# Layer 0's last stage: p is loaded, turned and split within the down-projection's last steps, and gates are closed one block product into the next group

## The chip, the core and the metric

The kernel runs on one core of one Trainium2 chip. The metric is the device time of one execution in microseconds. A second figure, the span, is the time from the first to the last instruction that the profile of one execution shows; a little time lies around it.

## What is computed

Two layers of a decoder trunk, for 512 tokens of 1024 features, all in float32. Each layer mixes tokens, then applies a gated MLP with a short convolution, and ends with an embedding that is added for each layer. The change lies at the seam of the last two parts of layer 0:

```python
def _conv_ffn(h, w_up, conv_w, conv_b, w_down):
    u = _causal_depthwise_conv(h @ w_up, conv_w) + conv_b
    gate, up = jnp.split(u, 2, axis=-1)
    return (jax.nn.gelu(gate, approximate=False) * up) @ w_down

def _per_layer_embedding(x, p_i, norm, w_gate, w_proj):
    gate = jax.nn.sigmoid(_rms_norm(x, norm) @ w_gate)
    return gate * (p_i @ w_proj)

# in the loop over the layers i
    x = x + _conv_ffn(_rms_norm(x, ffn_norm[i]), ffn_w_up[i], ffn_conv_w[i], ffn_conv_b[i], ffn_w_down[i])
    x = x + _per_layer_embedding(x, p[i], ple_norm[i], ple_w_gate[i], ple_w_proj[i])
```

Here `w_down` is 2816 x 1024, `w_gate` 1024 x 1024, `w_proj` 256 x 1024, and `p[i]` 512 x 256.

## The kernel before, in words

**Layout.** The residual x lies transposed in SBUF, as eight blocks `xT[m]` of 128 features by 512 tokens. Every product is made of float32 numbers cut in two: a high part (ScalarE copies to the rounded type fp32r) and the rest (VectorE subtracts). A product then takes three matmuls, high by high, high by low and low by high (`mm3`, lines 165 to 171, or the inner `product` of `seven`, lines 884 to 886). The helpers of such cuts are `split` (lines 108 and 109, or 111 and 112 with a gain), `cut` (149 and 150) and `cut_blocks` (825 and 826).

**Order.** The kernel is written for a framework whose planner lays out each engine's queue. Under `manual_schedule(engines={ET.PE})` TensorE's queue keeps the written order. The queues of VectorE, ScalarE, GpSimd and SP are ordered by the planner, which gives the earlier written instruction the preference among those whose inputs and buffers it expects to be ready. `high_priority(offset=n)` moves a block of instructions n places forward in that preference. Each queue then runs strictly in its order. Buffers belong to tags with a fixed number of slots: `raw` (fresh weights, 2 slots), `wh` and `wl` (cut weights, 3 each), `R` (2), `four` (7), `rs` (4), and two sets of PSUM banks, `ps` and `pa`, of 4 each. A load into a slot waits until the last reader of the slot's old contents is through.

**Block products.** A 2 x 2 product of blocks is done with seven half-sized products instead of eight (`seven`, line 870). One call handles a pair of output blocks X and Y, each 128 features by 512 tokens, and is a generator: TensorE's program takes it up to a `yield` and may put other work there. In order: W (weights `plain`, operand `e1`), copied by ScalarE into the left halves of X and Y (lines 890, 891); V (`t13`, `s1`), copied out by line 897 when asked; `o1` into X's left half and `s2` (weights `t2`) into Y's left half; a copy to X's right half (line 900); `s3` into it; a copy to Y's right half (line 903); `s4` into Y and `o2` into X. Each of the seven has 12 matmuls of 128 x 256. The weights' forms are made by `seven_forms` in this order: `plain` is cut (line 843); two subtractions (849, 850); `t13` is cut; a subtraction (857); `t2` is cut at a preference 40 places forward, into the `sq` slots that the sums of squares use; a subtraction (860). The last form is cut in `seven` itself (line 901).

**The down-projection** (`down`, line 1116) runs a plan of 16 steps for layer 0. The last two (steps 14 and 15 of 0 to 15) are the products of output blocks 6 and 7 with three activation blocks each: 18 matmuls of 128 x 512 a step. Then line 1210 adds the banks to `xT[6]` and `xT[7]`, and `finish` calls `blocks` (line 293), which scales each block by the norm's gain (299), cuts it, forms the sums that `seven` needs (314 to 318), cuts those, and adds the block's squares to the norm's sum (290, 291).

**The embedding of layer 0** (`ple0`, line 1311) follows. p is loaded in two halves into `R` slots (`p_halves`, line 1289, issued on SP); one of these slots holds the low part of activation block 7 until step 13 of the down-projection has used it. Then come the load of gate group 0's weights (line 1323), its forms, the load of the projection's weights into a `raw` slot (line 1336) and their split in two column halves (line 1339). Under the manual order for TensorE stand `load_p` (eight transposes of p, line 1305, and two splits of the result, called pT), the products `proj(0)` and `proj(1)`, and the loop over four gate groups of two feature blocks each. Group g issues the load of group g + 1, runs the seven products, and puts between them: in group 0 `end_norm` (line 333: transposes of the squares, line 330, a sum, line 339, and a reciprocal root on GpSimd, line 179) and `spread` (line 343: four transposes, line 348, and a copy, line 350, which make R); in the others two `proj`. Then it closes the gates: three VectorE operations with R (lines 1385, 1387, 1388), and for each block a sigmoid (1391), a product with proj (1392), an addition to `xT` (1393) and the squares. In the last group `enter` cuts the finished blocks for layer 1's first product. Layer 1's mixer follows.

The short lines that a sentence can't carry, of the loop before the change:

```python
                next(steps)
                if g == 0:
                    R = self.spread()
                else:
                    pjs.append(proj(2 * g + 1))
                last = steps
                if not ends:
                    steps = prepare(raw)
                X, Y, more = next(last)
```

Of the kernel before, what the change touches and what calls it, by code (L numbers as in the profile page):

```python
# [14 lines left out]
AF = mybir.ActivationFunctionType  # L15
ALU = mybir.AluOpType
# [3 lines left out]
P = 128  # L20
# [43 lines left out]
class Kernel:  # L64
# [802 lines left out]
        left, right = HALVES  # L867
        return dict(e1=part(0, left), o1=part(1, left), o2=part(1, right), s1=s1, s2=s2, s3=s3, s4=s4)

    def seven(self, od, ws, x, keep=None):  # L870


        nc = self.nc
        H = S // 2
        mm = nc.tensor.matmul
        W, V = self.pa(), self.pa()[:, :H]
        X, Y = self.ps(), self.ps()
        plain, t13, t2 = ws

        def product(out, w, c, x, first=False):  # L880
            kw = dict(skip_group_check=True)
            for j in range(ND // 2):
                (wh, wl), (xh, xl) = w(j, c), x(j)
                mm(out, wh, xh, start=first and j == 0, stop=False, **kw)  # L884
                mm(out, wh, xl, start=False, stop=False, **kw)  # L885
                mm(out, wl, xh, start=False, stop=j == ND // 2 - 1, **kw)  # L886

        left, right = HALVES
        product(W[:, left], plain, 0, x["e1"], True)
        nc.scalar.copy(X[:, left], W[:, left])  # L890
        nc.scalar.copy(Y[:, left], W[:, left])
        yield
        product(V, t13, 0, x["s1"], True)
        more = V
        if keep is not None:
            more = keep()
            nc.scalar.copy(more, V)
        product(X[:, left], plain, 1, x["o1"])
        product(Y[:, left], t2, 0, x["s2"])
        yield nc.scalar.copy(X[:, right], Y[:, left])  # L900
        last = self.cut_blocks(od)
        product(X[:, right], t13, 1, x["s3"])
        yield nc.scalar.copy(Y[:, right], X[:, right])
        product(Y[:, left], last, 1, x["s4"])
        product(X[:, right], last, 0, x["o2"])
        yield X, Y, more

    def ffn(self, i, project, next_gain):


        nc, a, tc = self.nc, self.a, self.tc
# [5 lines left out]
        with tc.tile_pool(name=f"ffn{i}", bufs=1) as fp:  # L917
            self.mlp = fp
            kept, acts, fours = [None] * NF, [None] * NF, []
# [104 lines left out]
            down_forms = []  # L1024
# [23 lines left out]
            operands = self.tokens_and_forms(xg, self.forms)  # L1048
# [8 lines left out]
            with tc.manual_schedule(engines={ET.PE}):  # L1057
                late = begin(0, steps, w0c)
                close = lambda: None
                for d in range(groups):  # L1060
                    g, y = both(), both()
                    copied = next(steps)
# [6 lines left out]
                    copied = next(steps)  # L1069
# [37 lines left out]
            work = [lambda f=f: split_blocks(f) for f in (14, 16, 18, 20)]  # L1107
            for f in (8, 10, 12):
                split_pair(f)
            self.down(i, acts, down_forms, both, work, finish, copied)  # L1110
            if i == 0:
                self.ple0(fp, both, self.g_mix[1])
            else:
                self.ple1(fp)

    def down(self, i, acts, forms, both, work, finish, copied):


        nc, tc = self.nc, self.tc
        H = S // 2  # L1120
# [190 lines left out]
    def ple0(self, fp, both, next_gain):  # L1311


        nc, a, tc = self.nc, self.a, self.tc
        H = S // 2
        forms = self.forms
        wg = a["ple_w_gate"][0].rearrange("(k p) n -> p k n", p=P)
        operands = {q: (lambda j, q=q: forms[j][q]) for q in ("e1", "o1", "o2", "s1", "s2", "s3", "s4")}
        groups = ND // 2

        def load(g):
            raw = self.raw(ND, 2 * P)
            nc.sync.dma_start(raw, wg[:, :, 2 * P * g : 2 * P * (g + 1)])
# [12 lines left out]
        nc.sync.dma_start(wj_raw, a["ple_w_proj"][0].rearrange("(k p) n -> p k n", p=P))  # L1336
        wj = [self.four(fp).rearrange("p a b -> p (a b)").rearrange("p (k n) -> p k n", k=2) for _ in range(2)]
        for c in (slice(0, D // 2), slice(D // 2, D)):
            self.split([w[:, :, c] for w in wj], wj_raw[:, :, c])

        def proj(m):
            pj = self.pa()
            c = slice(m * P, (m + 1) * P)
            for k in range(2):
                self.mm3(pj, [w[:, k, c] for w in wj], pT[k], start=k == 0, stop=k == 1)
            return pj

        def enter(*ms):
            for m in ms:
                hl = self.pair(self.fp, "b0", "b1")  # L1350
                self.split(hl, self.xT[m], next_gain[:, m : m + 1])
                self.xg.append(hl)

        with tc.manual_schedule(engines={ET.PE}):
            pT = self.load_p(0, fp, pin)
            pjs = [proj(0), proj(1)]
            for g in range(groups):
                ends = g + 1 == groups
                if not ends:
                    raw = load(g + 1)  # L1360
                next(steps)
                if ends:
                    enter(0, 1)
                next(steps)
                if ends:
                    enter(2, 3)
                if g == 0:
                    self.end_norm()
                    self.begin_norm(None)
                else:  # L1370
                    pjs = [proj(2 * g)]
                next(steps)
                if g == 0:
                    R = self.spread()
                else:
# [8 lines left out]
                h2 = lambda x: x.rearrange("p (u t) -> p u t", u=2)  # L1384
                nc.vector.tensor_tensor(gates[:, 0], X, R, ALU.mult)
                s = gates[:, 1]
                nc.vector.tensor_tensor(h2(s), h2(Y), more.unsqueeze(1).to_broadcast([P, 2, H]), ALU.add)
                nc.vector.tensor_tensor(s, s, R, ALU.mult)
                for c in range(2):
                    m, s = 2 * g + c, gates[:, c]  # L1390
                    nc.scalar.activation(s, s, AF.Sigmoid)
                    nc.vector.tensor_tensor(s, s, pjs[c], ALU.mult)
                    nc.vector.tensor_tensor(self.xT[m], self.xT[m], s, ALU.add)
                    self.squares(m)
            enter(6, 7)
        self.end_norm()

# [650 lines left out]
```

## Time and profile before

| what | value |
|---|---|
| median of 3 runs | 1211.22 us (1210.53 to 1211.4) |
| the profiled execution's own time | 1211.32 us |
| its span | 1209.5 us, 20223 instructions |
| mean granted TensorE clock | 0.996 |
| TensorE (matmul) busy | 1192.0 us, 99% |
| VectorE busy | 993.3 us, 82% |
| ScalarE busy | 691.6 us, 57% |
| GpSimd busy | 45.3 us, 4% |
| DMA | 117.76 MB, mean 97 GB/s |

How to read it. The profile calls TensorE PE (and its weight loads PEld), VectorE DVE, ScalarE ACT, GpSimd POOL and SyncE SP. "L1305" is line 1305 of the kernel. "out<-in" names tiles by the program's names, so `ps` and `pa` are PSUM banks and `wh<-raw` is a cut of fresh weights. Times in the timeline count from the span's start. An entry such as "[3.95 <-ACT four L108]" says that the engine sat idle for 3.95 us before this instruction, and that what ended the wait was ScalarE's instruction of line 108 that writes a tile `four`. The granted clock is the share of TensorE's full clock that the chip allowed. Matmuls are pipelined, so the step from one start to the next is what a matmul costs, not its own length. The seam that the change touches lies at 500 to 600 us.

### The profile page before, as it was taken

How to read it: one execution, taken by the hardware profiler on the slowest of the kernel's cores; microseconds unless marked ns; L12 is line 12 of the kernel's file. 1: busy time of each engine (PE TensorE's matmuls, PEld its weight loads, DVE VectorE, ACT ScalarE, POOL GpSimd, SP SyncE). 2: the span in 40 equal slices, each digit the busy share in tenths (PEclk: the TensorE clock that was granted, in tenths of full speed). 3: DMA queues.
4: the chain of work that ended last, by engine and by line, in shares of the span. 5: the costliest groups of instructions: out<-in, count | busy, mean ns of one | idle time of the engine just before them, and what ended most of it. 6: DMA issues, size and time to landing. Idle time of an engine off the chain costs nothing.

```text
span 1209.5 us, 20223 instructions
## 1 busy us (share of the span) xinstructions
PE 1192.0 (99%) x8218; PEld 1081.0 (89%) x8218; DVE 993.3 (82%) x1593; ACT 691.6 (57%) x1135; POOL 45.3 (4%) x64
## 2 busy tenths in 40 slices
PE   9999999999999999979999999999999999999998
PEld 8887789999999889859978988889999999888887
DVE  6786687898999986868769876687989999988595
ACT  7466565655565644745673564555565656645374
POOL 2600000000000000000100000000000000000000
PEclk9999999999999999989999999999999999999999
DMA  7232222323232433231321322223333333422601
GB/s 221 76 101 70 73 88 70 120 91 119 92 110 83 148 122 96 67 108 61 114 93 47 93 71 70 87 70 105 106 105 105 103 107 97 139 88 96 209 1 70
DMA packets 112928, 117.76 MB, mean 97 GB/s; under 512 B 2840, under 2 KB 107858, under 8 KB 112836
## 3 DMA queue, kind: packets, MB, share of 16 engines
q1 hardware_dynamic: 112000, 115.88, 29.8%
q8 instruction: 64, 1.05, 0.4%
q0 software_dynamic: 560, 0.42, 0.3%
q14 instruction: 28, 0.23, 0.1%
q10 hardware_dynamic: 276, 0.18, 0.0%
HBM read 114.37 MB, written 2.10 MB: 96 GB/s over the span
## 4 chain that ended last, share of the span: by engine, by line
PE 60%; issue 29%; DVE 7%; ACT 2%; DMA 1%; POOL 0%; ACTq 0%; POOLq 0%; DVEq 0%
PE ps L169 10%; PE ps L171 10%; PE ps L170 10%; PE pa L170 4%; PE pa L171 4%; PE pa L169 4%; PE ps L884 3%; PE ps L886 3%; PE ps L885 3%; DVE wl L150 1%; PE ps L1446 1%; PE ps L1445 1%; PE ps L1444 1%; PE pa L886 1%; DVE wl L826 1%
## 5 line engine op out<-in xcount | busy, mean ns | idle before, releaser
L150 DVE TENSOR_TENSOR wl<-raw,wh 128x1024 fp32r<-128x1024 f32 (+4 forms) x142 | 163.0, 1149 | 41.6 <-ACT wh L149 41.1
L149 ACT ACTIVATE wh<-raw 128x1024 fp32r<-128x1024 f32 (+4 forms) x142 | 141.4, 998 | 87.1 <-PE ps L170 55.5
L825 ACT ACTIVATE wh<-raw 128x1024 fp32r<-128x1024 f32 x90 | 95.8, 1065 | 125.1 <-DVE raw L850 76.1
L826 DVE TENSOR_TENSOR wl<-raw,wh 128x1024 fp32r<-128x1024 f32 x90 | 110.2, 1224 | 28.9 <-ACT wh L825 28.8
L938 DVE SCALAR_TENSOR_TENSOR zt<-z,vfa,zt 128x510 f32<-128x510 f32 (+1 forms) x176 | 131.2, 746 | 0.3
L171 PE MATMUL pa<-b,wl 128*128 128x256 f32 x352 | 97.3, 276 | 0.1
L171 PE MATMUL pa<-a,wl 128*128 128x256 f32 x352 | 97.3, 276 | 0.0
L169 PE MATMUL pa<-a,wh 128*128 128x256 f32 x352 | 97.2, 276 | 0.0
L170 PE MATMUL pa<-b,wh 128*128 128x256 f32 x352 | 97.2, 276 | 0.0
L169 PE MATMUL pa<-b,wh 128*128 128x256 f32 x352 | 97.2, 276 | 0.0
L170 PE MATMUL pa<-a,wh 128*128 128x256 f32 x352 | 97.2, 276 | 0.0
L936 ACT ACTIVATE zt<-z,vfb 128x512 f32<-128x512 f32 x88 | 71.6, 813 | 18.6 <-DVE z L928 9.3
L169 PE MATMUL ps<-b,wh 128*128 128x512 f32 x192 | 76.6, 399 | 0.0
L170 PE MATMUL ps<-b,wh 128*128 128x512 f32 x192 | 75.1, 391 | 0.0
L171 PE MATMUL ps<-b,wl 128*128 128x512 f32 x192 | 75.0, 390 | 0.0
L171 PEld LDWEIGHTS pa<-b,wl 128*128 128x128 f32 x352 | 66.1, 188 | 0.2 <-DVE wl L150 0.2
L169 PEld LDWEIGHTS pa<-b,wh 128*128 128x128 f32 x352 | 66.1, 188 | 0.0
L170 PEld LDWEIGHTS pa<-a,wh 128*128 128x128 f32 x352 | 66.1, 188 | 0.0
L170 PEld LDWEIGHTS pa<-b,wh 128*128 128x128 f32 x352 | 66.1, 188 | 0.0
L169 PEld LDWEIGHTS pa<-a,wh 128*128 128x128 f32 x352 | 66.1, 188 | 0.0
L171 PEld LDWEIGHTS pa<-a,wl 128*128 128x128 f32 x352 | 66.1, 188 | 0.0
L884 PE MATMUL ps<-four,wh 128*128 128x256 f32 x232 | 64.7, 279 | 0.0
(470 smaller groups left out, 3769.2 us busy)
## 6 DMA issues: line engine op xcount, KB each, us to landing
raw<-in_ffn_w_up_dram SPq DMA_DIRECT2D x42, 1024.0 KB, 5.0
raw<-in_ffn_w_down_dram SPq DMA_DIRECT2D x13, 1024.0 KB, 5.4
raw<-in_hy_w_in_dram SPq DMA_DIRECT2D x8, 1024.0 KB, 5.2
raw<-in_gla_w_in_dram SPq DMA_DIRECT2D x8, 1024.0 KB, 5.2
raw<-in_ffn_w_down_dram SPq DMA_DIRECT2D x8, 768.0 KB, 4.9
raw<-in_ple_w_gate_dram SPq DMA_DIRECT2D x6, 1024.0 KB, 5.2
raw<-in_hy_w_out_dram SPq DMA_DIRECT2D x16, 256.0 KB, 4.2
raw<-in_gla_w_out_dram SPq DMA_DIRECT2D x4, 1024.0 KB, 5.0
```

The costliest lines, as they stand in the source:

```text
L149: nc.scalar.activation(hv, v, AF.Copy)
L150: self.rest_cut = nc.vector.tensor_tensor(lv, v, hv.bitcast(F32), ALU.subtract)
L169: mm(out, lh, rh, start=start, stop=False, **kw)
L170: mm(out, lh, rl, start=False, stop=False, **kw)
L171: mm(out, ll, rh, start=False, stop=stop, **kw)
L825: nc.scalar.activation(h, src, AF.Copy)
L826: nc.vector.tensor_tensor(l, src, h.bitcast(F32), ALU.subtract)
L884: mm(out, wh, xh, start=first and j == 0, stop=False, **kw)
L885: mm(out, wh, xl, start=False, stop=False, **kw)
L886: mm(out, wl, xh, start=False, stop=j == ND // 2 - 1, **kw)
L936: nc.scalar.activation(y, z, AF.Identity, scale=w2[:, f : f + 1], bias=bb[:, f : f + 1])
L938: nc.vector.scalar_tensor_tensor(out=y[:, tap:], in0=z[:, : S - tap], scalar=w[:, f : f + 1], in1=y[:, tap:], op0=ALU.mult, op1=ALU.add,)
```

## The change

Four things are done, all in layer 0.

- The load of p is called at the beginning of step 14 of the down-projection, and the transposes and splits of p, with them a Sigmoid of four columns into a spare buffer, at the beginning of step 15. Layer 0's `ple0` takes the result instead of calling these itself.
- `spread` moves from behind the third part of group 0's products (after `s3`) to behind the last (`o2`).
- The gates of group g are closed after the first product W of group g + 1, those of the last group after the loop and after `enter(4, 5)`.
- The ScalarE copies within `seven` get a preference 60 places forward, in `ple0` alone.

In group 0 the order of `end_norm` and in the other groups that of the two `proj` stays.

```diff
-    def seven(self, od, ws, x, keep=None):
+    def seven(self, od, ws, x, keep=None, swift=False):
...
+        def copy(out, src):
+            with self.tc.high_priority(offset=60) if swift else nullcontext():
+                return nc.scalar.copy(out, src)
...
-        nc.scalar.copy(X[:, left], W[:, left])
-        nc.scalar.copy(Y[:, left], W[:, left])
+        copy(X[:, left], W[:, left])
+        copy(Y[:, left], W[:, left])
...
-            nc.scalar.copy(more, V)
+            copy(more, V)
...
-        yield nc.scalar.copy(X[:, right], Y[:, left])
+        yield copy(X[:, right], Y[:, left])
...
-        yield nc.scalar.copy(Y[:, right], X[:, right])
+        yield copy(Y[:, right], X[:, right])
...
-            self.down(i, acts, down_forms, both, work, finish, copied)
+            ahead = []
+            if i == 0:
+
+                def turned():
+                    self.pT = self.load_p(0, fp, self.pin)
+                    nc.scalar.activation(self.few(4, "rs", 4), self.mhalf[:, :4], AF.Sigmoid)
+
+                ahead += [lambda: setattr(self, "pin", self.p_halves(0)), turned]
+            self.down(i, acts, down_forms, both, work, finish, copied, ahead)
...
             for t, (u, name, k0, k1, s) in enumerate(plan):
+                if ahead and t + 2 >= len(plan):
+                    ahead.pop(0)()
...
-            return self.seven(od, self.seven_forms(ev, od, raw), operands, lambda: result()[:, :H])
-
-        pin = self.p_halves(0)
+            return self.seven(od, self.seven_forms(ev, od, raw), operands, lambda: result()[:, :H], True)
+
+        pT = self.pT
         steps = prepare(load(0))
...
+        def close(g, sums, pjs):
+            X, Y, more = sums
+            gates = both()
+            h2 = lambda x: x.rearrange("p (u t) -> p u t", u=2)
+            nc.vector.tensor_tensor(gates[:, 0], X, R, ALU.mult)
+            s = gates[:, 1]
+            nc.vector.tensor_tensor(h2(s), h2(Y), more.unsqueeze(1).to_broadcast([P, 2, H]), ALU.add)
+            nc.vector.tensor_tensor(s, s, R, ALU.mult)
+            for c in range(2):
+                m, s = 2 * g + c, gates[:, c]
+                nc.scalar.activation(s, s, AF.Sigmoid)
+                nc.vector.tensor_tensor(s, s, pjs[c], ALU.mult)
+                nc.vector.tensor_tensor(self.xT[m], self.xT[m], s, ALU.add)
+                self.squares(m)
+
+        late = None
         with tc.manual_schedule(engines={ET.PE}):
-            pT = self.load_p(0, fp, pin)
             pjs = [proj(0), proj(1)]
             for g in range(groups):
...
                 next(steps)
+                if late:
+                    close(*late)
                 if ends:
                     enter(0, 1)
                 next(steps)
                 if ends:
                     enter(2, 3)
...
                 next(steps)
-                if g == 0:
-                    R = self.spread()
-                else:
+                if g:
                     pjs.append(proj(2 * g + 1))
                 last = steps
                 if not ends:
                     steps = prepare(raw)
...
-                X, Y, more = next(last)
-                if ends:
-                    enter(4, 5)
-                gates = both()
...
+                late = g, next(last), pjs
+                if g == 0:
+                    R = self.spread()
+            enter(4, 5)
+            close(*late)
             enter(6, 7)
```

More of the change, by code (lines that the diff above doesn't have):

```diff
@@ L1114, in ffn, with down @@
                 self.ple1(fp)
-    def down(self, i, acts, forms, both, work, finish, copied):
+    def down(self, i, acts, forms, both, work, finish, copied, ahead=None):
         nc, tc = self.nc, self.tc
@@ L1366, in ple0 @@
                     enter(2, 3)
-                if g == 0:
+                if g:
+                    pjs = [proj(2 * g)]
+                else:
                     self.end_norm()
                     self.begin_norm(None)
-                else:
-                    pjs = [proj(2 * g)]
                 next(steps)
-                if g == 0:
-                    R = self.spread()
-                else:
+                if g:
                     pjs.append(proj(2 * g + 1))
@@ L1379, in ple0 @@
                     steps = prepare(raw)
-                X, Y, more = next(last)
-                if ends:
-                    enter(4, 5)
-                gates = both()
[L1384 to L1394, printed above, removed]
+                late = g, next(last), pjs
[3 more added lines that the diff above has]
+            close(*late)
             enter(6, 7)
```

## The prediction, made before the changed kernel was run

> **What bounds the kernel now.** I read the list of waits of TensorE first, because TensorE is busy 99% of the span: only its idle time can be won. These are its longest waits (engine and line, what it waited for, us in total, times, longest).
>
> ```profile
> PE pa L169 <- ACT four L108: 3.9, 1, 3.9
> PE pa L170 <- DVE four L109: 3.2, 1, 3.2
> PE pa L348 <- POOL rtok L179: 1.6, 1, 1.6
> ...
> PE ps L884 <- ACT ps L890: 0.9, 1, 0.9
> ...
> PE ps L884 <- ACT ps L900: 0.6, 1, 0.6
> ```
>
> All five lie in the stage that the change touches. The windows view cuts that stage at TensorE's own marks: the start of p's transposes, the start of gate group 0's first block product W, the ends of groups 0 to 3. Columns: length, then busy time and count of TensorE, its weight loads, VectorE, ScalarE, GpSimd; granted clock, DMA share, GB/s.
>
> ```profile
> 520.23:534.09 13.86, 6.69 (x21) 4.88 (x20) 10.68 (x19) 6.67 (x12) 0.00 (x0) 0.66 0.36 117
> 534.09:547.05 12.96, 11.31 (x93) 10.87 (x92) 5.53 (x8) 4.43 (x8) 1.43 (x1) 0.97 0.11 38
> 547.05:560.54 13.49, 12.62 (x98) 11.91 (x97) 11.90 (x17) 9.22 (x15) 0.00 (x0) 1.00 0.23 78
> 560.54:573.21 12.67, 12.58 (x98) 11.72 (x97) 11.54 (x18) 7.08 (x13) 0.00 (x0) 1.00 0.21 61
> 573.21:586.81 13.60, 13.05 (x100) 12.20 (x99) 13.09 (x20) 10.52 (x19) 0.00 (x0) 1.00 0.23 64
> ```
>
> The first row holds 8 transposes and the 12 matmuls of proj(0) and proj(1), and takes 13.86 us at a granted clock of 0.66. The timeline of TensorE shows why (start, length, instruction, idle time before it).
>
> ```profile
> 519.77 0.39 PE L170 MATMUL ps<-four,wh 128*128 128x512 f32 x1
> 520.00 0.39 PE L171 MATMUL ps<-four,wl 128*128 128x512 f32 x1
> 520.23 1.03 PE L1305 MATMUL pa<-cf,pin 128*128 128x128 f32 x8
> 525.21 0.79 PE L169 MATMUL pa<-four,four 128*128 128x512 f32 x1 [3.95 <-ACT four L108]
> 529.23 0.79 PE L170 MATMUL pa<-four,four 128*128 128x512 f32 x1 [3.23 <-DVE four L109]
> ...
> 533.66 0.63 PE L171 MATMUL pa<-four,four 128*128 128x512 f32 x1
> 534.09 0.41 PE L884 MATMUL pa<-a,wh 128*128 128x256 f32 x1
> ...
> 535.12 0.28 PE L884 MATMUL pa<-b,wh 128*128 128x256 f32 x1
> ```
>
> Two things are to be seen. TensorE waits for pT, which ScalarE and VectorE split only behind the last feature blocks. And after the waits a 512-wide matmul starts 0.43 us after the one before (533.66 to 534.09), against 0.23 (519.77 to 520.00): the idle time costs a slow restart too.
>
> **The removed waits.** (A) At the fast spacing the 12 matmuls take 12 x 0.23 = 2.76 us, the transposes 1.03; the stage is 13.86 long, so 10.07 are idle or slow. W's first six matmuls take 1.03 (534.09 to 535.12) instead of some 6 x 0.115 = 0.69: 0.34 more. A = 10.4 us. The change puts the transposes and pT's split ahead of the down-projection's last step (18 matmuls, 18 x 0.23 = 4.1 us), which covers two 0.58 us splits on ScalarE and two 0.69 on VectorE, if they come first there.
>
> ```profile
> 541.89 0.28 PE L886 MATMUL ps<-b,wl 128*128 128x256 f32 x1
> 543.81 0.65 PE L348 MATMUL pa<-cf,rtok 128*128 128x128 f32 x4 [1.64 <-POOL rtok L179]
> ...
> 549.66 0.28 PE L886 MATMUL pa<-b,wl 128*128 128x256 f32 x1
> 550.81 0.39 PE L884 MATMUL ps<-a,wh 128*128 128x256 f32 x1 [0.87 <-ACT ps L890]
> ```
>
> (B) spread waits for the reciprocal root: 543.81 - 541.89 - 0.11 of step = 1.8 us. It moves behind s4 and o2, 24 matmuls x 0.114 = 2.7 us of cover, so 1.8 goes. What is late next is R's copy, needed only by the close in group 1, which has a product to spare.
>
> (C) The left half of X in group 1 waits 0.87 (1.0 by the starts) because the copies L890 and L891 stand behind group 0's sigmoids and their table load on ScalarE. Closing after the next group's W, with the copies raised, puts them first. The sigmoids come some 0.7 us later, and nothing on TensorE reads them. (D) The 0.6 us wait for L900 in group 3 is of the same kind. I take both as gone, bound 0 to 1.6.
>
> Together: 10.4 + 1.8 + 1.0 + 0.6 = 13.8 us. The profiled execution took 1211.32 (span 1209.5 plus 1.8 around it; the median of the three runs is 1211.22, so the two agree). With nothing given back: 1197.5.
>
> **What it adds.** (1) A wait ahead of the last step. The second half of p is loaded into the buffer that the last B step (ended 512.07) frees, behind the projection weights in SP's queue.
>
> ```profile
> 511.93 0.37 SPq L1336 DMA_DIRECT2D raw<-in_ple_w_proj_dram  x1
> 512.35 1.98 SPq L1289 DMA_DIRECT2D pin<-in_p_dram  x1
> 528.05 3.30 SPq L1323 DMA_DIRECT2D raw<-in_ple_w_gate_dram  x2
> ```
>
> The trace's answer on that load of pin alone ends with
>
> ```profile
> DMA to landing us min/median/max: 5.6/5.6/5.6
> ```
>
> so it lands at 512.35 + 5.6 = 517.95. The buffer cannot come free earlier, so calling the load earlier in the program does not move it. The transposes would now start at 516.15, where the last step starts today; the first four (0.5 us, data long there) end at 516.7, and the other four wait 1.3 us. Behind them in TensorE's queue stand the last step's 18 matmuls, and behind those the additions L1210 and the last two blocks. Bounds: 0, if pin's issue goes ahead of the projection weights (another pin load landed in 2.7), and 1.3, if the order stays. I take 1.3, the row's own value. Behind pin on SP stands only the gate load of 528.05, so the issue pushes nothing.
>
> (2) Group 1's weights. Its gate load is issued at 528.05, when VectorE has read the last of the projection weights' buffer; it then takes 5.2 us to land:
>
> ```profile
> 526.75 1.22 DVE L109 TENSOR_TENSOR four<-raw,four 128x1024 fp32r<-128x1024 f32 x1
> ```
>
> ```profile
> raw<-in_ple_w_gate_dram SPq DMA_DIRECT2D x6, 1024.0 KB, 5.2
> ```
>
> So the second half of that split, which the planner set 6.6 us after the end of the last step (520.2), holds the load. Today nothing suffers, since W of group 1 starts at 547. In the changed kernel call E the end of the last step: W of group 1 starts at E + 2.76 + 7 products of 1.37 + two sets of transposes of 0.6 = E + 13.5. If the split keeps its place, it starts near E + 6 (one operation ahead of it, L860, can now run before E) and ends at E + 7.2; the load lands at E + 12.5. Then this chain follows:
>
> ```profile
> 555.54 0.69 DVE L849 TENSOR_TENSOR raw<-raw 128x512 f32<-128x512 f32 x1
> 556.26 0.69 DVE L850 TENSOR_TENSOR raw<-raw 128x512 f32<-128x512 f32 x1
> 556.99 1.06 ACT L825 ACTIVATE wh<-raw 128x1024 fp32r<-128x1024 f32 x1
> 558.08 1.23 DVE L826 TENSOR_TENSOR wl<-raw,wh 128x1024 fp32r<-128x1024 f32 x1 [1.12 <-ACT wh L825]
> ```
>
> First cut 1.06 + 1.23, L849 and L850 1.4, second cut 1.06 + 1.23: 6.0 us to t13's low half, at E + 18.5. V of group 1 wants it at E + 13.5 + 1.4 + 0.2 = E + 15.1. The stall is 3.4; I take 3.5. Bounds: 0, if the planner puts that split ahead of L1210, and 4.1, if it keeps 6.6. The row it is nearest to is the order of today. Smaller stalls before it (V of group 0 may wait up to 1.0 for the last blocks' sums) shorten it by as much and are not added.
>
> (3) The Sigmoid on four columns is there to load ScalarE's table early.
>
> ```profile
> 547.87 1.28 ACT L1391 ACT_TABLE_LOAD   x1
> 549.17 1.32 ACT L1391 ACTIVATE zt<-zt 128x512 f32<-128x512 f32 x2
> ```
>
> ```profile
> 0.73 0.14 POOL L695 MEMSET pad<- 128x2 f32 x2 [0.29 <-POOLq L2034]
> ```
>
> The row in the second fence, from GpSimd's timeline, is a memset written for a convolution some 67 us into the kernel: the planner put it first, since it waits for nothing. The small Sigmoid waits for nothing either, so it probably goes far ahead, before Gelu calls, and the load stays with the first gates. Bounds: ScalarE gains 1.28, or loses two loads, 2.6, somewhere where it is idle a good part of the time; for TensorE I take 0, since (C) has the copies in front anyway.
> The Trainium skill, "ScalarE: Activation LUTs", section "What ACT_TABLE_LOAD costs", gives a change of set 1.28 us plus a drain of about 1.38, 2.66 in all, and its section "Table sets: the hidden batching unit" has one set active at a time. The trace shows 1.28, and the sigmoid starting at once (547.87 + 1.28 = 549.15): the measurement decides. By the page the misplaced Sigmoid would cost ScalarE up to 5.3 us, still off TensorE's path.
>
> (4) The closes. Their VectorE operations keep their number and nearly their place, as X and Y are done only when the next group's W begins. The last close stays where it is. Cost 0; without cover, at most the 0.6 us of one operation per group.
>
> **Sum:** 1211.32 - 13.8 + 1.3 + 3.5 = **1202.3 us**.
>
> **Rivals.** First, the **group 1 load is early** and nothing else binds: 1211.32 - 13.8 + 1.3 = 1198.8. For it: TensorE's end moves back by 1.0 + 1.3 us, so VectorE has time ahead of L1210; against it, pT's two low halves (0.6 us each) now stand there.
>
> Second, **VectorE becomes the bound**. Over 520.23 to 586.81 it is busy 10.68 + 5.53 + 11.90 + 11.54 + 13.09 = 52.7 us; less 1.2 for pT, 51.5 remain. TensorE's path would be 66.6 - 1.0 - 13.8 = 51.8 us. VectorE would have to be 99% busy; the densest stage shows 13.09 / 13.60 = 96%. At 95% it needs 54.2, 2.4 more than TensorE: 1198.8 + 2.4 = 1201.2. Against it: the closes may trail into the next layer's first products.
>
> Third, **slower**: pin's second half is issued behind the gate load of 528.05 in SP's queue. It then lands near 531. TensorE has stood for 14 us, and the 18 matmuls, most of them at 0.43 us, take 6.7: E is 531.0 + 0.5 + 6.7 = 538.2, W starts at 541.0 instead of 534.1. Less the 0.34 and B to D (3.7), the kernel is 3.2 us slower: 1214.5. It turns to a loss when pin lands after about 527.8, ten microseconds later than now. Against it: pin is issued 16 us before that load today and has no reason to fall behind it.
>
> Fourth, the change **does only part of what it says**: pT's splits stay behind the last blocks, as now, because the planner orders them. Then only the transposes, B, C and D move, 1.0 + 3.4 us, and with (1) the time is 1211.32 - 4.4 + 1.3 = 1208.2.
>
> **How the numbers follow.** Forecast (late group 1 weights) 0.42; early and unbound 0.22; VectorE the bound 0.22; part only 0.07; slower 0.07. The range goes from 1197.3, just under the sum with nothing given back, to 1206.0: the forecast with the upper bound of (2), 0.6 more, plus a second stall of some 3 us of the same kind, say half in group 0 and half at the next layer. A measurement of this kernel can tell about 0.2%, 2.4 us: faster is under 1208.8, slower above 1213.6. Faster 0.89: the first three cases and 0.03 of the fourth. Same 0.05: the rest of the fourth, and 0.01 of the third rival, where pin lands only somewhat late. Slower 0.06: the third rival otherwise.
>
> **What would show it.** pT's L169 no longer in TensorE's list of waits; L1305 starting near 516.2, its second four near 518; the granted clock back near 1.00 between 520 and 534; L348 without a wait for rtok, L890 without one before L884. For (2): a wait of W or V in group 1 for L825 or L826 of some 3.5 us, with the load's issue 7 us or more behind the last L171. For the rival: that issue within 3 us of it. For (3): an L1391 table load still there. The forecast is wrong if TensorE keeps a wait above 4 us in this stage, or if time changes outside 510 to 610 us.

## The result and the profile after

| kernel | median | lowest to highest | runs |
|---|---|---|---|
| before, on the same chip | 1210.95 us | 1210.53 to 1211.4 | 4 |
| changed | 1203.15 us | 1201.69 to 1203.31 | 4 |

The ratio is 0.9933, with a 95% interval of 0.9916 to 0.995: faster by 7.8 us. The profiled execution took 1203.05 us, its span is 1201.2 (1209.5 before).

TensorE is still busy 99% of the span. The list of its waits in the changed kernel (line, what it waited for, us in total, times, longest) answers the list that the prediction began with:

```profile
PE pa L204 <- DVE mhalf L193: 1.3, 1, 1.3
PE pa L889 <- DVE b L109: 1.1, 1, 1.1
PE pa L1319 <- DMA pin<-in_p_dram: 1.1, 1, 1.1
PE ps L888 <- ACT ps L882: 1.0, 3, 0.5
PE pa L888 <- ACT b L108: 0.7, 1, 0.7
```

The two waits for pT (7.1 together), the one for `rtok` and the one for the copies at the head of group 1 are gone. (The first line is another place of the kernel. The old lines 884 to 886 are now 888 to 890, line 1305 is now 1319, and all copies within `seven`, the old lines 890, 891, 897, 900 and 903, now stand at line 882.) New are a wait for the second half of p, which the prediction had, and two for `b` at lines 888 and 889. `b` holds the cut block sums, so this is the product V of gate group 0.

The windows view of the changed kernel cuts the same stages: p's transposes to W of group 0, then groups 0 to 3. Columns: length, busy time and count of TensorE, weight loads, VectorE, ScalarE, GpSimd; granted clock, DMA share, GB/s.

```profile
516.02:525.01 8.99, 7.93 (x39) 6.49 (x38) 7.40 (x10) 6.60 (x10) 0.00 (x0) 1.00 0.11 36
525.01:540.41 15.40, 13.12 (x94) 12.29 (x92) 11.85 (x20) 6.92 (x13) 1.43 (x1) 0.89 0.43 137
540.41:552.92 12.51, 12.51 (x99) 11.88 (x97) 10.94 (x16) 9.06 (x15) 0.00 (x0) 1.00 0.26 84
552.92:565.45 12.53, 12.53 (x98) 11.69 (x97) 11.97 (x18) 7.37 (x13) 0.00 (x0) 1.00 0.21 61
565.45:578.39 12.94, 12.70 (x98) 11.72 (x97) 12.86 (x20) 10.30 (x19) 0.00 (x0) 1.00 0.19 59
```

The first row now includes the 18 matmuls of the down-projection's last step, and runs at a full clock. Beside the rows of before: W of group 0 starts at 525.01 instead of 534.09, which is 9.08 earlier. Group 0 has become longer, 15.40 instead of 12.96, though it lost a wait of 1.8. Groups 1, 2 and 3 are shorter by 0.98, 0.14 and 0.66 (0.34 of the last is two matmuls of the next layer that ran ahead of this mark before and no longer do). In sum: -9.08 + 2.44 - 0.98 - 0.14 - 0.66 = -8.4 us at the end of the stage, -8.1 without those 0.34; the span is 8.3 shorter. Outside this stage little changes.

So the one surprise sits in group 0. TensorE's timeline of the changed kernel shows it:

```profile
527.30 0.28 PE L890 MATMUL pa<-b,wl 128*128 128x256 f32 x1
528.25 0.38 PE L888 MATMUL pa<-b,wh 128*128 128x256 f32 x1 [0.67 <-ACT b L108]
529.73 0.38 PE L889 MATMUL pa<-b,wh 128*128 128x256 f32 x1 [1.10 <-DVE b L109]
529.95 0.28 PE L890 MATMUL pa<-b,wl 128*128 128x256 f32 x1
...
530.90 0.30 PE L889 MATMUL ps<-b,wh 128*128 128x256 f32 x1
531.01 0.40 PE L890 MATMUL ps<-b,wl 128*128 128x256 f32 x1
531.21 0.42 PE L888 MATMUL ps<-b,wh 128*128 128x256 f32 x1
...
537.21 0.39 PE L888 MATMUL ps<-a,wh 128*128 128x256 f32 x1 [0.50 <-ACT ps L882]
```

Three losses can be read off. V's last three matmuls need `s12` of the last pair of blocks: from 527.30 to 529.73 pass 2.43 us, in which two steps of 0.11 belong, so 2.2 are lost. Then, from 530.9 on, each matmul starts 0.21 after the one before instead of 0.115: the clock has fallen to half (the granted clock of 531.01 to 534.41 is 0.50), for about 16 matmuls, 1.6 us. Last, a copy costs 0.7 by the starts. Together 4.5, and 12.96 - 0.34 - 1.8 + 4.5 = 15.3: this accounts for the row of 15.40 of the profiled execution.

### The profile page after: what moved, and what is told of

Its sections match the earlier page's. It is cut to its first block, busy times and chain, and to the rows that moved or that the text cites. A ratio compares the mean times of both kernels' runs of the same rounds, so it can differ in the third digit from the quotient of the medians.

```text
span 1201.2 us, 20217 instructions
## 1 busy us (share of the span) xinstructions
PE 1190.4 (99%) x8218; PEld 1080.6 (90%) x8218; DVE 993.5 (83%) x1593; ACT 690.8 (58%) x1137; POOL 45.3 (4%) x64
## 4 chain that ended last, share of the span: by engine, by line
PE 85%; DVE 9%; ACT 3%; DMA 1%; issue 1%; ACTq 0%; POOL 0%; SPq 0%; DVEq 0%
PE ps L169 12%; PE ps L170 11%; PE ps L171 11%; PE pa L170 7%; PE pa L171 6%; PE pa L169 6%; PE ps L888 5%; PE ps L890 5%; PE ps L889 5%; PE pa L889 2%; PE pa L890 2%; PE pa L888 2%; DVE wl L150 1%; DVE wl L826 1%; PE ps L1465 1%
```

## The experiments

**Theory** at this point: the change does what the prediction's (A) to (D) say; the rest is V's wait for `s12`, caused by cuts of weights that ScalarE and VectorE do ahead of it, and the half clock behind it. **Rivals**: that one part of the change does it all; that the wait for p (1.1) is what is left to win; that group 1's late weights, which the prediction counted on, still cost something; that VectorE is simply full; that the new small Sigmoid costs time. In e4, e5 and e9 the line numbers of `seven` are 2 to 3 higher than in the changed kernel; e1 is built on the kernel before and has that kernel's. The experiments ran on three chips, so each is given with the kernel before that ran beside it.

### Each part alone

e1 takes the edits of `down` and `pT` alone (the closes stay where they were), e2 the closes and raised copies alone:

```diff
 # e1_ahead_only, on the kernel before
+            ahead += [lambda: setattr(self, "pin", self.p_halves(0)), turned]
+            self.down(i, acts, down_forms, both, work, finish, copied, ahead)
...
-        pin = self.p_halves(0)
+        pT = self.pT
...
-            pT = self.load_p(0, fp, pin)
```

> The kernel before, with p loaded, turned and split in the last two steps of the down-projection, and nothing else: spread, the closes and the copies stay as they were. Theory (the gain is pT's wait, 9.1 us, less what comes behind it): the changed kernel's 1203.2 plus the waits that only the other part removes, 1.8 for the reciprocal root and about 1.4 in groups 1 to 3, so 1206.4, with TensorE's wait for rtok and for L890 in the list again. Rival (the later closes carry most of the gain): 1209 or more. Rival (VectorE is the bound, so that either part alone gives nearly all): 1203.

```diff
 # e2_close_only, on the changed kernel
-            self.down(i, acts, down_forms, both, work, finish, copied, ahead)
+            self.down(i, acts, down_forms, both, work, finish, copied)
...
-        pT = self.pT
+        pin = self.p_halves(0)
...
+            pT = self.load_p(0, fp, pin)
```

> The changed kernel with p turned where it was before, in the embedding itself: only spread, the closes and the copies are changed. Theory: the waits B, C and D go, 1.8 + 1.0 + 0.6 less what the rest of group 0 hides, so 1207.7, with pT's two waits of 3.9 and 3.2 still at the head of TensorE's list. Rival (closes carry the gain): 1204. Rival (VectorE is the bound): no gain, 1211.

Measured: e1 1204.92 us, ratio 0.9951 (0.9936 to 0.9966); e2 1209.13, ratio 0.9983 (0.9974 to 0.9992); the kernel before beside them 1210.65. So 5.7 and 1.5 us, 7.2 together, where both at once brought 7.8. Neither median is where it was expected: e1 is 1.5 below 1206.4, e2 1.4 above 1207.7, and what moves them is not shown. The waits divide as they should. In e1:

```profile
PE pa L348 <- POOL rtok L179: 1.3, 1, 1.3
...
PE pa L885 <- DVE b L109: 1.1, 1, 1.1
...
PE ps L884 <- ACT ps L890: 0.9, 1, 0.9
PE pa L884 <- ACT b L108: 0.7, 1, 0.7
```

The spread's wait and the copies' wait are still there; V's waits for `b` have come in with the early p, not with the closes. In e2 it is the other way round: pT's waits of 3.9 and 3.5 are back, those two are gone.

### V's wait for the block sums

e4 holds the cut of the last form and that of `t2` back until ScalarE (and for `t2` VectorE too) has cut `s12`:

```diff
 # e4_blocks_first, on the changed kernel
-        with self.tc.high_priority(offset=40):
+        with self.tc.high_priority(offset=40), ExitStack() as held:
+            for x in behind or ():
+                held.enter_context(self.tc.issue_after(x.ins))
             t2 = self.cut_blocks(b11, False)
...
-        last = self.cut_blocks(od)
+        with self.tc.issue_after(behind[0].ins) if behind else nullcontext():
+            last = self.cut_blocks(od)
...
+        steps = prepare(load(0), self.sums_split)
```

> The changed kernel with two cuts of group 0's weights held back: the cut of the last form and that of t2 are queued behind the split of the last blocks' sums s12 on ScalarE and VectorE. Theory (V of group 0 waits 2.2 us since ScalarE does the last form's cut, 1.06 us, ahead of the last blocks, and the slow clock of 530.9 to 534.4 follows from this wait): V's wait falls to 0.5 or less, the clock stays up, 1203.2 - 1.7 - 1.6 = 1199.9. Rival (the clock falls on its own): 1201.5. Rival (the cuts are then late for s2 and s4 instead): 1203.

Measured: 1200.4 us (1199.56 to 1201.11), ratio 0.9916 (0.99 to 0.9933); the kernel before beside it 1210.65. That is 0.5 above the expected time. What had stood in the way is seen on ScalarE in the changed kernel. Line 825 is a cut of weights, 299 the scaling of a finished block, 108 the high parts of the block sums:

```profile
522.31 1.06 ACT L825 ACTIVATE wh<-raw 128x1024 fp32r<-128x1024 f32 x1 [2.39 <-PE ps L170]
523.28 0.71 ACT L299 ACTIVATE zt<-xT,vec 128x512 f32<-128x512 f32 x1
...
526.38 0.61 ACT L825 ACTIVATE t<-raw 128x512 fp32r<-128x512 f32 x1
526.89 0.62 ACT L882 COPY ps<-pa 128x256 f32<-128x256 f32 x2
527.56 0.63 ACT L108 ACTIVATE b<-zt 128x512 fp32r<-128x512 f32 x1
```

and on VectorE, where line 826 is t2's low part and 109 those of `s12` and `s34`:

```profile
528.39 0.69 DVE L826 TENSOR_TENSOR t<-raw,t 128x512 fp32r<-128x512 f32 x1
528.99 1.29 DVE L109 TENSOR_TENSOR b<-zt,b 128x512 fp32r<-128x512 f32 x2
```

The cut of the last form starts at 522.31, and the first finished block is scaled only behind it, at 523.28; t2's low part goes ahead of that of `s12`. In e4 TensorE's timeline has

```profile
527.37 0.39 PE L891 MATMUL pa<-b,wh 128*128 128x256 f32 x1 [0.25 <-ACT b L108]
528.22 0.38 PE L892 MATMUL pa<-b,wh 128*128 128x256 f32 x1 [0.46 <-DVE b L109]
```

The two waits are 0.71 together, a little over the 0.5 that was expected. Group 0 takes 12.71 us, with the granted clock at 1.00:

```profile
524.56:537.27 12.71, 11.49 (x93) 10.66 (x92) 11.00 (x19) 7.27 (x13) 1.43 (x1) 1.00 0.48 166
```

So the place of two cuts in the queues costs 2.7 us of group 0 in these two profiles: 1.06 of it as listed waits, and nearly all the rest as the half clock, which comes in some executions only (see below). By its median e4 is the fastest of the kernels tried, with e9 within its spread. Its four runs lie below the changed kernel's four (from 1201.69, beside a kernel before of 1210.95).

### Group 1's weights, which the prediction counted on

e7 puts the second half of the projection weights' split on VectorE where the prediction expected it, behind the last blocks' sums:

```diff
 # e7_split_late, on the changed kernel
-            self.split([w[:, :, c] for w in wj], wj_raw[:, :, c])
+            with tc.issue_after(self.last_sum.ins) if c.start else nullcontext():
+                self.split([w[:, :, c] for w in wj], wj_raw[:, :, c])
```

> The changed kernel with the second half of the projection weights' split on VectorE held behind the sums of the last block, the place that the prediction's step (2) assumed. Theory (that place holds back group 1's gate load): the load is issued some 5 us later than the 524.3 of the changed kernel, W or V of group 1 waits for a weight cut by about 3 us, and a slow clock may follow; 1203.2 + 3.5 = 1206.7, up to 1208.5 with the clock. Rival (the delay is hidden, since group 0 got longer by itself): 1203.2.

e3 gives the second half of p a buffer of its own, so that its load needn't wait for the last B step:

```diff
 # e3_own_slot, on the changed kernel
+        if pool is not None:
+            pin[1] = pool.tile([P, NT, P], F32, tag="z", name=self.nm("pin"), bufs=3)
```

> The changed kernel with the second half of p in a slot of another tag that is long free, so that its load can be issued early. The wait for pin (1.06 us) goes. Theory: this alone doesn't pay, because with TensorE's last step earlier the planner puts the second half of the projection weights' split behind the last blocks' sums; group 1's gate load then comes late and W or V of group 1 waits some 3.5 us, as step (2) of the prediction had it: 1203.2 - 1.1 + 3.5, less up to 2 us of the waits in group 0 that the other order spares, 1204 to 1205.5. Rival (waits add up one by one): 1202.1.

Measured: e7 1205.4 us, ratio 0.9953 (0.9939 to 0.9967), the kernel before beside it 1211.16; e3 1205.72, ratio 0.9958 (0.9943 to 0.9973), beside 1210.65. e7 is 1.3 below the expected 1206.7, e3 0.2 above its range. Both miss their rivals (1203.2 and 1202.1) by more than 2 us. SP's queue shows when the gate load for group 1 is issued. In the changed kernel:

```profile
512.22 0.46 SPq L1303 DMA_DIRECT2D pin<-in_p_dram  x1
524.34 20.39 SPq L1337 DMA_DIRECT2D raw<-in_ple_w_gate_dram  x3
```

In e3 there is no load of p at 512 any more, and the wait for it is gone, but the planner, with other slots to reckon with, also moved the split by itself:

```profile
511.56 0.37 SPq L1353 DMA_DIRECT2D raw<-in_ple_w_proj_dram  x1
528.79 2.12 SPq L1340 DMA_DIRECT2D raw<-in_ple_w_gate_dram  x2
```

The load is 4.45 us later. TensorE then stands in V of group 1, and the clock falls behind that:

```profile
537.91 0.28 PE L890 MATMUL pa<-b,wl 128*128 128x256 f32 x1
540.70 0.58 PE L888 MATMUL pa<-a,wh 128*128 128x256 f32 x1 [2.52 <-ACT wh L825]
541.08 0.41 PE L889 MATMUL pa<-a,wh 128*128 128x256 f32 x1
541.96 0.58 PE L890 MATMUL pa<-a,wl 128*128 128x256 f32 x1 [0.47 <-DVE wl L826]
```

```profile
536.31:555.36 19.05, 16.07 (x100) 14.91 (x98) 15.26 (x21) 10.32 (x16) 0.00 (x0) 0.82 0.17 57
```

Group 1 takes 19.05 instead of 12.51: 3.4 us of waits by the starts, and about 2.7 of half clock. In e7, where the load goes out at 529.34, three smaller waits for cut weights appear (0.29 and 0.53 in group 1, 0.91 in group 3), group 1 takes 14.03, and V's two waits of group 0 stay as in the changed kernel (0.67 and 1.10); in e3, whose planner also put the last form's cut behind `s12`, they are 0.52 and 0.35. So late weights make group 1 longer by 1.5 us in e7's profile and by 6.5, with the half clock, in e3's. The changed kernel doesn't pay this, because its planner put that split early.

### All of it together

e9 is e3 and e4 at once, with both halves of the split raised so that the load goes out early:

```diff
 # e9_all_three, on e3 and e4
+            with tc.high_priority(offset=300):
+                self.split([w[:, :, c] for w in wj], wj_raw[:, :, c])
```

> The changed kernel with the second half of p in a slot of its own, the two late cuts behind the last blocks, and the split of the projection weights raised 300 places so that the planner keeps it ahead of the last blocks' sums. Theory (the waits are three separate ones, and with all three covered none takes their place): no wait for pin, V of group 0 waits under 0.5, no wait for weights in group 1, clock near 1.00 throughout: 1200.4 - 0.9 = 1199.5 or a little less, 1198.5 at best. Rival (VectorE is the bound by then): 1200.4 or more.

Measured: 1200.55 us (1199.99 to 1202.9), ratio 0.9919 (0.9905 to 0.9932), the kernel before beside it 1211.16: no better than e4, as the rival had it and not the theory. The gate load goes out at 521.39, the wait for p is gone, and W of group 0 starts at 523.96, 0.6 ahead of e4. But TensorE waits for the block sums longer instead:

```profile
527.72 0.38 PE L891 MATMUL pa<-b,wh 128*128 128x256 f32 x1 [1.07 <-ACT b L108]
528.59 0.39 PE L892 MATMUL pa<-b,wh 128*128 128x256 f32 x1 [0.49 <-DVE b L109]
```

e4 reaches this point at 528.22 and e9 at 528.59. e9's VectorE shows why (line 109 is the split of the projection weights, both halves at once, and 1226 the additions of the last two blocks):

```profile
519.01 2.35 DVE L109 TENSOR_TENSOR four<-raw,four 128x1024 fp32r<-128x1024 f32 x2
...
521.88 1.27 DVE L1226 TENSOR_TENSOR xT<-xT,ps 128x512 f32<-128x512 f32 x2
```

In e4 the additions start at 521.58, before the last step's end (521.84); in e9 they start 0.7 after it (521.17), because VectorE is still busy, with the raised split and behind it the last split of pT. From there on the finish of the last two blocks on ScalarE and VectorE sets the time, and by what TensorE arrives earlier it waits longer. So without the wait for p nothing was won here, and the rival that this wait is what is left to win falls for this order. What it would be worth with the additions in time is not shown, since e9 changes VectorE's order too.

### The half clock

e5 puts nine extra matmuls ahead of V's last three in group 0, as work for TensorE in the wait. They write a bank that nothing reads.

```diff
 # e5_fill, on the changed kernel
+        def filler():
+            ps = self.ps()
+            for _ in range(9):
+                nc.tensor.matmul(ps, wj[0][:, 0, :P], pT[0][0], start=True, stop=True)
```

> The changed kernel with nine extra matmuls of 128x512 (9 x 0.23 = 2.0 us, into a bank that nothing reads) ahead of the last three matmuls of group 0's product V, so that TensorE is busy while it would wait for the last blocks' sums. Theory (the half clock of 530.9 to 534.4 comes from the 2.2 us of standing still just before it): V ends where it did, near 530.1, the granted clock stays near 1.00 behind it, and the time falls by the slow stretch, to 1201.6. Rival (the clock falls for another reason, or the order of the other engines costs the time): 1203.2 or more, with the same slow stretch.

Measured: 1202.77 us (1201.55 to 1204.02), ratio 0.9931 (0.9917 to 0.9944), the kernel before beside it 1211.16. The profiled execution, 1201.55, is as expected, the median is not. In its profile no wait for `b` is listed, the clock is 1.00 in group 0, which takes 13.73, but the median is that of the changed kernel within its spread: for the time this is inconclusive. One explanation is that the half clock doesn't come in every execution. e7 had already shown the same two waits, 0.67 and 1.10, with the clock at 1.00 behind them. So the changed kernel was run with a profile twice more, and e7 once, with nothing edited:

> The changed kernel, unaltered, looked at once more. Question: is the fall of TensorE's clock behind V of group 0's two waits (0.67 and 1.10 us) fixed by the program, or does it come in some executions only? If fixed: the granted clock of 530 to 534 is near 0.6 again and the time is 1203.0 to 1203.4. If it comes and goes: in a profile without it the sixteen matmuls from about 530.9 on stand 0.113 us apart, and the time is some 1.6 lower, 1201.3 to 1201.8, near the fastest of the four runs (1201.69).

> The same once more. Fixed by the program: as the first, to 0.3 us in the place and length of the fall. Comes and goes: the time goes with the fall, 1203.2 +- 0.4 with it and 1201.6 +- 0.4 without.

> The kernel with the second half of the projection weights' split held behind the last block, unaltered, looked at once more; its first profile had the same two waits (0.67 and 1.10 us) and no fall, at 1204.14, the fastest of four (to 1206.89). Fixed by the program: no fall again, 1204 to 1204.5. Comes and goes: a fall in this profile is as likely as not, and with it the time is 1205.5 to 1206.9.

Measured: 1202.01, 1201.57 and 1206.16 us, one execution each; the kernel before beside them 1209.72. Group 0 of the changed kernel in the first repeat and in the second:

```profile
524.38:539.79 15.41, 13.13 (x93) 12.29 (x92) 11.89 (x20) 6.93 (x13) 1.43 (x1) 0.89 0.42 137
```

```profile
525.15:539.00 13.85, 11.56 (x93) 10.73 (x92) 11.49 (x20) 6.99 (x13) 1.43 (x1) 1.00 0.46 153
```

The waits are the same in both (0.68 and 1.09, 0.68 and 1.10). With the fall the group takes 15.41, as in the first profile; without it 13.85. So the fall comes and goes in the same program, and costs group 0 1.55 us. The expected time was missed for the first repeat: it had the fall and yet 1202.01, not 1203.0 or more. But the kernel before, too, took 1209.72 here instead of 1210.95, and TensorE came to p's transposes at 515.41 in the first repeat, at 516.39 in the second and at 516.02 in the first profile. So a single time doesn't tell the two cases apart; the length of group 0 does. The repeated e7 had the fall this time (group 0: 15.41, against 13.74 before) and took 1206.16 against 1204.14. Of seven profiles with these two waits (three of the changed kernel, e1, e6, e7 twice) five have the fall. Of the five kernels whose profiled group 0 has other waits (e2, e3, e4, e5 and e9) none has it there; that the two waits bring it is likely by this, and not proved.

Nor is the fall all that differs between executions. A fall of 3.4 us at half clock takes 1.7 / 1201 = 0.0014 off the mean granted clock of a run, so a run with a mean of 1.000 had none. Of the four runs of the changed kernel two have 1.000, and they took 1201.69 and 1203.31 us. What makes these 1.6 us is not known.

### The small Sigmoid

e6 leaves out the Sigmoid on four columns, whose result nothing uses:

```diff
 # e6_no_sigmoid, on the changed kernel
-                    nc.scalar.activation(self.few(4, "rs", 4), self.mhalf[:, :4], AF.Sigmoid)
```

> The changed kernel without the small Sigmoid. Theory (the planner set it at 193 us, before the Gelu calls, so it saves nothing): the table load of 1.28 us stays with the first gates, the one at 193 us is gone, and the time is 1203.2 within 0.7. Rival (its presence matters in either direction): a change of 1.3 or more.

Measured: 1202.6 us (1201.47 to 1204.24), ratio 0.993 (0.9917 to 0.9944), the kernel before beside it 1211.16: no difference that these runs can tell. In the changed kernel ScalarE's timeline has the line at

```profile
193.00 1.28 ACT L1119 ACT_TABLE_LOAD   x1
194.29 0.21 ACT L1119 ACTIVATE rs<-mhalf 128x4 f32<-128x4 f32 x1
```

some 320 us ahead of where it is written, and the load that it should have brought forward is still in group 1:

```profile
543.32 1.28 ACT L1378 ACT_TABLE_LOAD   x1
544.61 0.63 ACT L1378 ACTIVATE zt<-zt 128x512 f32<-128x512 f32 x1
```

It does nothing for the gates, and costs nothing that can be seen.

## Why the prediction came close, and which step of it was wrong

The forecast was 1202.3 us and the median is 1203.15. But the terms didn't all come as predicted, and that the sum did is in part luck:

| term | predicted | measured in the profile |
|---|---|---|
| W of group 0 starts: (A) and (1) | 534.09 - 10.07 + 1.3 = 525.32 | 525.01 |
| group 0: W's first six faster, (B) | -2.14 | +2.44 |
| group 1: (C), and (2) | -1.0 + 3.5 = +2.5 | -0.98 |
| group 2 | 0 | -0.14 |
| group 3: (D) | -0.6 | -0.66, -0.32 without the two moved matmuls |

**(A), right.** The transposes start at 516.02, the last step covers pT's splits, and the twelve matmuls of the two projections take 2.72 us; W's first six take 0.70.

**(1), right, with the row's own value.** Predicted 1.3, listed 1.06: p was issued at 512.22 and landed 5.4 us later, at 517.6. In the profiles of the other kernels that load p so, the wait is between 0.7 and 1.3.

**(C), right**: the copies ahead of group 1's left half have no wait. **(B), right in the wait, but not in the gain**: line 348 has no wait any more, but the copy to Y's right half (537.21, 0.50 listed, 0.7 by the starts) now has one in its place. In the kernel before this copy ran at 542.26, while TensorE stood waiting for `rtok`; with `spread` moved away nothing covers it. All profiles with `spread` behind `o2`, e2 among them, show this wait of 0.50 in group 0; the kernel before and e1 don't. So 1.1 of the 1.8 remain, and the prediction had put the 0.7 at nothing. e1 shows that the waits of (B) and (C) return without the closes' part. **(D), half right**: of 0.6 some 0.3 came back, and three waits for line 882, 1.0 together, remain over the kernel.

**(2), wrong, and this is the step that failed.** The prediction held that the second half of the projection weights' split keeps its place behind the last blocks, and so holds group 1's load; it took "the order of today". In the changed kernel the planner placed it at 523.10, right behind the additions to `xT`, 0.8 us after the last step's end (522.29). The load went out 2.05 us after that end, not 7, and group 1 has no wait for weights. On VectorE (line 1222 is the additions, 109 the second half of the split):

```profile
521.81 1.37 DVE L1222 TENSOR_TENSOR xT<-xT,ps 128x512 f32<-128x512 f32 x2
523.10 1.22 DVE L109 TENSOR_TENSOR four<-raw,four 128x1024 fp32r<-128x1024 f32 x1
```

A load that goes out within 3 us of that end is the sign the prediction had given for its first rival, the early load. e3 and e7 show that the mechanism itself is real where the order is the other.

In its place stood what the prediction had mentioned in half a sentence, with a bound: V of group 0 "may wait up to 1.0" for the last blocks' sums. It measured 2.2, and it was counted as covered by the stall of (2). The bound is about what the order of before gives. There the additions end at 521.46, 1.2 after the last step's end (520.23), and the low half of `s12` is done at 526.5, 5.0 later:

```profile
520.18 1.28 DVE L1210 TENSOR_TENSOR xT<-xT,ps 128x512 f32<-128x512 f32 x2
...
525.22 1.29 DVE L109 TENSOR_TENSOR b<-zt,b 128x512 fp32r<-128x512 f32 x2
```

V needs it 2.7 + 2.4 = 5.1 after the step's end; 1.2 + 5.0 - 5.1 gives 1.1. After the change these steps take 6.5 us (523.18 to 529.7), because the planner rearranged both engines: on ScalarE the last form's cut went ahead of both scalings, where before a cut of this size stood behind them and behind `s12`:

```profile
526.06 1.05 ACT L825 ACTIVATE wh<-raw 128x1024 fp32r<-128x1024 f32 x1
```

e4 gave 1.06 of the listed waits back by that order alone, and by the starts it loses 1.15 (526.85 to 528.22, less two steps), about what the order of before gives.

And one thing was not foreseen at all: the half clock behind the two waits, 1.55 us of group 0 in those executions that have it. The prediction knew the price of a fall from the stage of before, and didn't ask whether the waits that remain could cause one.

So 2.2 + 1.6 + 0.7 in group 0 stood in for the 3.5 in group 1. No step of the prediction ties the one to the other: that the two differ by 1.0 only is luck. With the terms as measured the prediction's own sum would have been 1211.32 - 13.8 + 1.1 + 4.5 = 1203.1, or 1203.4 with the 0.3 of (D) that did not come back; the profiled execution took 1203.05.

**The rivals.** *Load early and nothing else binding* (1198.8): the load was early, something else did bind. *VectorE the bound* (1201.2): VectorE is busy 12.86 of 12.94 us in group 3, so it is close there, but TensorE idles only 0.24 in that group. From the last step's end to the end of group 3 VectorE is busy 49.8 of 56.1 us, 89%, where the rival needed 95. So it did not bound the changed kernel; what TensorE waits for in group 0 is the place of a few operations in the queues. e4, with the same work, has it busy 49.8 of 53.5 us, 93%, and its 1200.4 is near the rival's time. Whether VectorE keeps e4 and e9 from going lower is open. *Slower* and *part only*: p's second half was issued 12 us ahead of the gate load, and the splits of pT ran beside the last step, so neither took place.

## What to carry to other kernels

Where a planner orders the queues, a change upstream rearranges them: a term that rests on an operation keeping its place needs both orders priced, with what each makes late. One can be paid in place of the other, as here the block sums in place of group 1's weights, or both at once, as in e7. An instruction that is moved can also have covered another's wait, as `spread` did for a copy: ask what stands bare when it has gone. When a stage is shortened, follow the producers of the first operand that is now needed early, on every engine, in order, before taking a bound for it. And price a wait of a TensorE-bound kernel with the slow stretch that may follow it: here 1.8 us of listed waits were followed by up to 1.55 more.

## What the runs showed of the hardware that was not expected

TensorE's granted clock fell to 0.50 although it had not been idle for longer than 1.4 us at a stretch just before: two idle stretches of 0.8 and 1.4 us, with one matmul between, were followed by the fall in five profiles of seven, and not in the other two. A single wait of 1.64 us, the one for `rtok` in the kernel before (543.81), was followed by full speed; one of 2.52 us in e3 (540.70) by matmuls at half speed until about 547.3. In the first repeat the slow steps run thus:

```profile
529.78 0.34 PE L888 MATMUL ps<-a,wh 128*128 128x256 f32 x1
529.91 0.42 PE L889 MATMUL ps<-a,wh 128*128 128x256 f32 x1
...
533.12 0.35 PE L889 MATMUL ps<-b,t 128*128 128x256 f32 x1
533.31 0.28 PE L890 MATMUL ps<-b,t 128*128 128x256 f32 x1
```

from about 529.8 to 533.2, some 3.4 us; in the first profile from 530.9 to about 534.3, as long, but beginning 1.2 us after V's last wait instead of 0.7. The Trainium skill, "TensorE: Matmul & The Clock Gate", section "Part 1: The HAM clock gate (the "warmup" mystery)", has the clock set by a window of about 3.4 us that runs freely, and half speed after at least one idle window. The length of the slow stretch agrees with that, and a free-running window would also explain that the same waits do and don't bring the fall. But no window of 3.4 us was idle throughout: by these profiles one that is idle for at most 2.2 us of it (0.8 + 1.4) can be enough, an estimate from the starts. From which share on, and that it is the window's position that decides, is argued here and not shown by a run.
